# FFN gate and up in a two-layer decoder trunk: x as the stationary operand in 512-column blocks, and the results turned to channels by 32x32 transposes and copies between quadrants

## The chip, the cores and the metric

The kernel runs on one core of a Trainium2 chip. Its engines work side by side, each on its own queue of instructions: TensorE (PE; PEld is its load of the stationary operand), VectorE (DVE), ScalarE (ACT), GpSimd (POOL) and SyncE (SP, which here issues most of the transfers). The metric is the time of one execution on the device, in microseconds. A difference of about 0.2% (5.5 us) is what a measurement of this kernel can tell from no change.

## The reference, cut to what matters

The trunk has two layers with different mixers. Behind each mixer stands the same gated FFN with a causal convolution of three taps over the 256 positions of the sequence, for each of its 5120 channels:

```python
D_MODEL, SEQ, DEPTH, D_FF, FFN_CONV = 2048, 256, 2, 5120, 3

def causal_dwconv(x, w):
    K = w.shape[0]
    L = x.shape[1]
    xp = jnp.pad(x, ((0, 0), (K - 1, 0), (0, 0)))
    return sum(xp[:, j:j + L] * w[j] for j in range(K))

def conv_glu(x, w_gate, w_up, conv_w, w_down):
    gate = causal_dwconv(x @ w_gate, conv_w)
    return (jax.nn.silu(gate) * (x @ w_up)) @ w_down

for i in range(DEPTH):
    h = gdn_mixer(...) if i == 0 else dsa_mixer(...)
    x = layer_norm(DN_ALPHA * x + h, ln1_g[i], ln1_b[i])
    f = conv_glu(x, ffn_w_gate[i], ffn_w_up[i], ffn_conv_w[i], ffn_w_down[i])
    x = layer_norm(DN_ALPHA * x + f, ln2_g[i], ln2_b[i])
    x = x + jax.nn.sigmoid(x @ ple_w_gate[i]) * (p[i] @ ple_w_proj[i])
```

## The kernel before

All inputs are float32. Each product is made of three products of rounded parts: a number is split into hi (rounded to the format that PE multiplies) and lo (what is left), and hi x hi, hi x lo and lo x hi are added up in PSUM.

Weights come as blocks of 512 KB, 128 partitions by 1024 numbers. For each block, `weigh` plans four steps: SP issues the load into `raw` (L418), ACT rounds it to `hi` (L424; the planner may give this to DVE as a cast, L428), DVE subtracts to `lo` (L432), and PE multiplies. There are three buffers each of raw, hi and lo; hi and lo of a block come free when PE has finished it. x, normed and transposed, stays in `xT`: for each of the 16 k (128 rows of the model dimension) hi and lo side by side, 2 x 256 positions.

`column` makes the blocks of some columns of a weight. It has two forms. In the wide form (`wide=True`, L347 to L357, 256 columns, blocks of 4 k) the weights are stationary: for each k and each 128 columns, one matmul of hi against the 512 numbers of x's hi and lo (L357), one of lo against the 256 of x's hi (L354). The result has channels on partitions; its two halves must be added. In the other form (512 columns, blocks of 2 k) x is stationary: for each k and each 128 positions, L367 and L368 multiply x's hi and x's lo with 512 columns of hi, and L370 x's hi with 512 columns of lo. The result has positions on partitions. The down product, the output products and some others have this form already. Gate and up are wide, since the convolution runs over positions, which must then lie in a row.

`ffn` plans what follows a column of gate and of up. For each 128 channels of gate: ACT copies one half of the result (`fold`, L1540), DVE adds the other and writes `fpd` (the join, L1542; two zeros stand in front), ACT multiplies by the last tap into `fac` (L1564), DVE adds the other two taps (L1567), ACT takes silu (L1570). For up: fold and join into `fh`, DVE multiplies with `fac` (L1583), ACT rounds the product into `hTA` or `hTB` (L1585), DVE subtracts for its lo (L1587). hTA and hTB are the stationary operand of down.

The order on each engine is set when the program is built. Every step is added to `Plan` with an engine, an assumed cost, its predecessors, the buffers that it takes and gives back, and a rank; `Plan.run` goes through an assumed time and takes for each engine the step that can start, by rank. Some steps name a second engine (`other`) that may take them. On the chip each engine keeps to that order. `rest` plans both layers from the output product of the mixer on: the norm (its pairs of k are turned by PE, L1473, and written to xT), gate and up in turn, the affine part of the norm on x (L1518), down, the norm behind it and the last product.

In the opening, x and the first four blocks come in pieces. Of x's first four k, one k, one k and two k; of the first block too, which ACT's queue loads while SP loads x. Four warm-up matmuls on zeros (`spin`, L270) go ahead on PE.

## Time and profile before

| | us |
|---|---|
| median of three runs | 2734.23 (2733.2 to 2734.66) |
| the profiled execution: its time | 2730.83 |
| its span in the profile | 2729.0 |
| PE busy in the span | 2718.1 |
| DVE busy | 1903.1 |
| ACT busy | 1464.6 |
| POOL busy | 236.2 |

The span is what the profile shows from the first to the last instruction; the execution's own time has 1.8 us around it. An engine's busy time is the union of its instructions. PE's instructions overlap (a matmul starts before the one in front has ended), so a matmul's rate is read from the starts of many in a row and not from the duration of one. The mean granted clock of TensorE was 0.999 of full speed.

### The profile page before, as it was taken

How to read it: one execution, taken by the hardware profiler on the slowest of the kernel's cores; microseconds unless marked ns; L12 is line 12 of the kernel's file. 1: busy time of each engine (PE TensorE's matmuls, PEld its weight loads, DVE VectorE, ACT ScalarE, POOL GpSimd, SP SyncE). 2: the span in 40 equal slices, each digit the busy share in tenths (PEclk: the TensorE clock that was granted, in tenths of full speed). 3: DMA queues.
4: the chain of work that ended last, by engine and by line, in shares of the span. 5: the costliest groups of instructions: out<-in, count | busy, mean ns of one | idle time of the engine just before them, and what ended most of it. 6: DMA issues, size and time to landing. Idle time of an engine off the chain costs nothing.

```text
span 2729.0 us, 39745 instructions
## 1 busy us (share of the span) xinstructions
PE 2718.1 (100%) x14686; PEld 2353.3 (86%) x14686; DVE 1903.1 (70%) x3077; ACT 1464.6 (54%) x2393; POOL 236.2 (9%) x415
## 2 busy tenths in 40 slices
...
DVE  7988789777787766666446866787766666655575
...
GB/s 245 230 253 174 183 185 187 196 177 165 171 184 177 212 199 201 205 199 191 194 194 240 149 195 208 182 151 193 167 189 197 193 198 193 196 193 190 213 173 189
DMA packets 415378, 527.56 MB, mean 193 GB/s; under 512 B 24848, under 2 KB 305280, under 8 KB 414928
## 3 DMA queue, kind: packets, MB, share of 16 engines
...
q10 hardware_dynamic: 560, 0.52, 0.1%
...
## 4 chain that ended last, share of the span: by engine, by line
PE 97%; DMA 1%; DVE 1%; POOL 1%; issue 0%; ACT 0%; ACTq 0%; SPq 0%; DVEq 0%
PE mm_ps L357 34%; PE mm_ps L354 18%; PE b_ps L367 13%; PE b_ps L370 13%; PE b_ps L368 13%; PE mm_ps L351 1%; PE o_ps L1266 1%; PE s_ps L1226 0%; PE n_ps L1473 0%; PE s_ps L1141 0%; PE o_ps L1265 0%; PE l_ps L919 0%; PE ot_ps L1305 0%; DMA raw<-in_gdn_w_in 0%; PE g_ps L1119 0%; PE s_ps L1242 0%
## 5 line engine op out<-in xcount | busy, mean ns | idle before, releaser
L432 DVE TENSOR_TENSOR lo<-raw,hi 128x1024 fp32r<-128x1024 f32 (+1 forms) x903 | 1099.8, 1219 | 664.1 <-ACT hi L424 653.2
L424 ACT ACTIVATE hi<-raw 128x1024 fp32r<-128x1024 f32 (+1 forms) x877 | 923.8, 1054 | 1069.1 <-PE mm_ps L357 454.6
L357 PE MATMUL mm_ps<-xT,hi 128*128 128x512 f32 x4056 | 991.6, 393 | 3.0 <-ACT hi L462 2.7
L357 PEld LDWEIGHTS mm_ps<-xT,hi 128*128 128x128 f32 x4056 | 741.7, 189 | 146.2 <-ACT hi L462 3.2
L354 PEld LDWEIGHTS mm_ps<-xT,lo 128*128 128x128 f32 x4056 | 522.2, 191 | 20.3 <-DVE lo L432 0.4
L354 PE MATMUL mm_ps<-xT,lo 128*128 128x256 f32 x4056 | 533.3, 283 | 0.2 <-DVE lo L432 0.2
L367 PE MATMUL b_ps<-hi,xT 128*128 128x512 f32 (+2 forms) x678 | 259.8, 384 | 0.0
L368 PE MATMUL b_ps<-hi,xT 128*128 128x512 f32 (+2 forms) x678 | 257.4, 380 | 0.0
L367 PE MATMUL b_ps<-hi,hTA 128*128 128x512 f32 x512 | 199.2, 389 | 0.0
L368 PE MATMUL b_ps<-hi,hTA 128*128 128x512 f32 x512 | 199.2, 389 | 0.0
L370 PE MATMUL b_ps<-lo,xT 128*128 128x512 f32 (+2 forms) x678 | 180.4, 382 | 0.0
L368 PEld LDWEIGHTS b_ps<-hi,xT 128*128 128x128 f32 x678 | 127.4, 188 | 22.8
L367 PEld LDWEIGHTS b_ps<-hi,xT 128*128 128x128 f32 x678 | 127.4, 188 | 22.8
L370 PEld LDWEIGHTS b_ps<-lo,xT 128*128 128x128 f32 x678 | 124.4, 188 | 22.6
L370 PE MATMUL b_ps<-lo,hTA 128*128 128x512 f32 x512 | 136.8, 389 | 0.0
L1512 POOL DMA_DIRECT2D lng<-in_ln_g x16 | 8.7, 543 | 1351.0 <-DVE x L1518 1267.1
L368 PEld LDWEIGHTS b_ps<-hi,hTA 128*128 128x128 f32 x512 | 96.1, 188 | 20.0
L367 PEld LDWEIGHTS b_ps<-hi,hTA 128*128 128x128 f32 x512 | 96.1, 188 | 20.0
L370 PEld LDWEIGHTS b_ps<-lo,hTA 128*128 128x128 f32 x512 | 96.1, 188 | 20.0
L367 PE MATMUL b_ps<-hi,oT 128*128 128x512 f32 (+1 forms) x258 | 102.2, 396 | 0.8 <-ACT hi L424 0.8
L368 PE MATMUL b_ps<-hi,oT 128*128 128x512 f32 (+1 forms) x258 | 100.3, 389 | 0.0
L598 DVE SCALAR_TENSOR_TENSOR ac<-pd,cw,ac 128x256 f32<-128x256 f32 x192 | 90.5, 481 | 3.3
...
## 6 DMA issues: line engine op xcount, KB each, us to landing
raw<-in_gdn_w_in SPq DMA_DIRECT2D x188, 512.0 KB, 4.3
raw<-in_ffn_w_down SPq DMA_DIRECT2D x160, 512.0 KB, 4.1
raw<-in_ffn_w_up SPq DMA_DIRECT2D x158, 512.0 KB, 4.1
raw<-in_ffn_w_gate SPq DMA_DIRECT2D x157, 512.0 KB, 4.2
raw<-in_dsa_w_in SPq DMA_DIRECT2D x72, 512.0 KB, 3.6
raw<-in_gdn_w_o SPq DMA_DIRECT2D x64, 512.0 KB, 4.0
raw<-in_ple_w_gate SPq DMA_DIRECT2D x56, 512.0 KB, 4.2
raw<-in_dsa_w_o SPq DMA_DIRECT2D x32, 512.0 KB, 4.4
```

The costliest lines, as they stand in the source:

```text
L351: nc.tensor.matmul(ps[o][:m, :S], (hi if kind == "hi" else lo)[:, k, o * P:o * P + m], xk[:, j], start=s and not j and kind == "hi", stop= ...
L354: nc.tensor.matmul(ps[o][:m, S:], lo[:, k, o * P:o * P + m], xk[:, 0], start=False, stop=e)
L357: nc.tensor.matmul(ps[o][:m], hi[:, k, o * P:o * P + m], xk.rearrange("p a b -> p (a b)"), start=s, stop=e)
L367: nc.tensor.matmul(ps[o][:, c], xh, hi[:, k, c], start=s, stop=False)
L368: nc.tensor.matmul(ps[o][:, c], xl, hi[:, k, c], start=False, stop=False)
L370: nc.tensor.matmul(ps[o][:, c], xh, lo[:, k, c], start=False, stop=e and c.stop == n)
L424: nc.scalar.activation(hi, box["raw"], AF.Copy)
L432: nc.vector.tensor_tensor(lo, box["raw"], box["hi"].bitcast(F32), op=ALU.subtract)
L598: nc.vector.scalar_tensor_tensor(box["ac"], box["pd"][:, k:k + S], wt[:, k:k + 1], box["ac"], op0=ALU.mult, op1=ALU.add)
L1266: nc.tensor.matmul(ps[:, h], qd()[:, h, a], u()[:, a, h], start=not a, stop=True)
L1512: d = add(G, 0.55, lambda r=r, src=src: nc.gpsimd.dma_start(out=r(), in_=bass.AP(tensor=src.tensor, offset=src.offset + nb * 512, ap=[[0, ...
```

## The change

Gate and up take the form with x stationary, in columns of 512: gate(n0) and up(n0) now make four times 128 channels each, from blocks of 2 k by 512 columns. The result has positions on partitions, 2 x 128 of them by 512 channels, in two PSUM banks. `turned` brings it to channels on partitions: DVE transposes each bank in blocks of 32x32 into `xb` (`flip`), and 16 copies of 32 partitions by 256 numbers move the blocks from quadrant b of the partitions to quadrant q of `fpd`, which holds four times 2 + 256 numbers a partition. The copies are planned half for DVE and half for ACT, each with the other engine as second choice. Behind them the taps stay at 256 numbers each; silu, the product with gate, the rounding and the subtraction take 1024 numbers at once. fpd exists once and serves gate and up in turn, fac once. fold and join go.

xb becomes one tile whose halves the norm and the last product use in turn (`half_`). The first gate and up columns of a layer run block by block in turn. The blocks that are made ahead of the first norm in layer 0 are planned at other places.

In the opening the pieces of x and of the first block are 2 k each (256 KB), and six warm-up matmuls run instead of four.

```diff
-                                fac=3, fh=2, xb=2, lng=1, lnb=1, qi=2, rl=2, qq=2, pr=2, prT=2, qs=1, ks=2)
+                                fac=1, fp=1, xb=2, lng=1, lnb=1, qi=2, rl=2, qq=2, pr=2, prT=2, qs=1, ks=2)
...
-        add(E, 3.6, lambda: spin(4, True), take=["bk"], give=["bk"], rank=-9)
+        add(E, 4.9, lambda: spin(6, True), take=["bk"], give=["bk"], rank=-9)
...
-            k1 = 4 * nb
-            for n in (2, 2) if nb else (1, 1, 2):
-                k0, k1 = k1, k1 + n
-                ks = slice(k0, k1)
+            n = 2
+            for k0 in range(4 * nb, 4 * nb + 4, n):
+                ks = slice(k0, k0 + n)
...
-                xs.extend([[f]] * n)
+                xs.extend([[f]] * (n // 2))
...
-                parts = ((0, 1), (1, 2), (2, 4)) if not i else ((0, 2), (2, 4))
-                for j, (j0, j1) in enumerate(parts):
...
-                        (nc.sync if i else nc.scalar).dma_start(out=box["raw"][:, j0:j1],
-                                          in_=b["src"][b["rows"] + j0 * P:b["rows"] + j1 * P, c0:c0 + n]
+                        (nc.sync if i else nc.scalar).dma_start(out=box["raw"][:, 2 * j:2 * j + 2],
+                                          in_=b["src"][b["rows"] + 2 * j * P:b["rows"] + (2 * j + 2) * P, c0:c0 + n]
...
-                    if i or j > 1:
-                        h.append(add(A, 0.13 + 0.25 * w, high, [d], take=["hi"] * (not j), rank=0, behind=h[:j] + xs[3] * (i == 1),
-                                     other=(V, 0.11 + 0.14 * w, cast, lambda: R["cast0"])))
+                    if i or j:
+                        h.append(add(A, 0.63, high, [d], take=["hi"] * (not j), rank=0, behind=h[:j] + xs[1] * (i == 1),
+                                     other=(V, 0.39, cast, lambda: R["cast0"])))
                     else:
...
-                if kind == "hi" and b is order[0]:
-                    r += [(kind, ks[:1]), (kind, ks[1:2]), (kind, ks[2:])]
-                    continue
...
+        xb = {}
+
+        def halves():
+            if id(self.area) not in xb:
+                xb[id(self.area)] = self.area, new("xb", [2, 512])
+            return xb[id(self.area)][1]
+
+        def half_():
+            xb["n"] = xb.get("n", 1) + 1
+            return halves()[:, xb["n"] % 2]
...
-            fp = [lazy(lambda n=n: new(f"fpd{n}", [2 + S])) for n in range(2)]
-
...
-            hT = lambda k: (w["hA"](k, 1) if k < 32 else w["hB"](k - 32, 1))[:, 0]
+            fp = lazy(lambda: new("fpd", [4, 2 + S]))
+            clear = add(G, 0.3, lambda: nc.gpsimd.memset(fp()[:, :, 0:2], 0.0), [opened])
+            hT = lambda k, n=1: w["hA"](k, n) if k < 32 else w["hB"](k - 32, n)
             G_, hd = {}, {}
+
+            def turned(state, task):
+                box, d, r = {}, [], []
+
+                def flip(a):
+                    if not a:
+                        box["t"] = halves()
+                    nc.vector.transpose(box["t"][:, a], state["ps"][a])
+                for a in range(2):
+                    d.append(add(V, 0.72, lambda a=a: flip(a), [task], take=["xb"] * 2 * (not a), give=["mm"], rank=1,
+                                 behind=d[:1]))
+
+                def ends(b, q):
+                    return (fp()[32 * q:32 * q + 32, :, 2:].rearrange("p t (o b i) -> p o t b i", b=4, i=32)[:, :, :, b],
+                            box["t"][32 * b:32 * b + 32].rearrange("p o (t q i) -> p o t q i", q=4, i=32)[:, :, :, q])
+
+                def move_v(b, q):
+                    nc.vector.tensor_copy(*ends(b, q))
+
+                def move_a(b, q):
+                    nc.scalar.activation(*ends(b, q), AF.Copy)
+                for b in range(4):
+                    for q in range(4):
+                        v, c = ((lambda f=f, b=b, q=q: f(b, q)) for f in (move_v, move_a))
+                        how = (V, 0.25, v), (A, 0.4, c)
+                        one, two_ = how if (b + q) % 2 else how[::-1]
+                        r.append(add(*one, [*d, clear], take=["fp"] * (not r), rank=1.5, behind=r[:1],
+                                     other=(*two_, lambda: R["move"])))
+                return r
 
             def gate(n0):
                 def done(state, task):
                     soon = marked()
-                    for n in range(2):
-                        pd, m = fp[n], n0 + n
-                        ac = lazy(lambda: new("fac", [S], 3))
-                        x = folded(state, n, task, lambda pd=pd: pd()[:, 2:], take=["pd"], more=[clear])
-                        x = add(A, 0.5, lambda pd=pd, ac=ac, m=m: nc.scalar.activation(
-                            ac(), pd()[:, 2:], AF.Identity, scale=w["taps"](2, m)), [x, w["cw"]], take=["fac"], rank=2)
+                    ac = lazy(lambda: new("fac", [4, S]))
+                    moved, x = turned(state, task), []
+                    for n in range(4):
+                        m = n0 + n
+                        y = add(A, 0.5, lambda ac=ac, n=n, m=m: nc.scalar.activation(
+                            ac()[:, n], fp()[:, n, 2:], AF.Identity, scale=w["taps"](2, m)), [*moved, w["cw"]],
+                            take=["fac"] * (not n), give=["xb"] * 2 * (not n), rank=2)
                         for k in (1, 0):
-                            x = add(V, 0.48, lambda k=k, pd=pd, ac=ac, m=m: nc.vector.scalar_tensor_tensor(
-                                ac(), pd()[:, k:k + S], w["taps"](k, m), ac(), op0=ALU.mult, op1=ALU.add), [x],
-                                give=["pd"] * (not k), rank=soon)
-                        G_[m] = add(A, 0.41, lambda ac=ac: nc.scalar.activation(ac(), ac(), AF.Silu), [x], rank=2,
-                                    table="silu"), ac
-                return column(t["ffn_w_gate"][i], 0, n0 * P, 256, KT, lambda k: self.xT[:, k], True,
+                            y = add(V, 0.48, lambda k=k, ac=ac, n=n, m=m: nc.vector.scalar_tensor_tensor(
+                                ac()[:, n], fp()[:, n, k:k + S], w["taps"](k, m), ac()[:, n], op0=ALU.mult, op1=ALU.add), [y],
+                                rank=soon)
+                        x.append(y)
+                    G_[n0] = add(A, 1.07, lambda ac=ac: nc.scalar.activation(ac(), ac(), AF.Silu), x, give=["fp"], rank=2,
+                                 table="silu"), ac
+                return column(t["ffn_w_gate"][i], 0, n0 * P, 512, KT, lambda k: self.xT[:, k], False,
             def up(n0):
                 def done(state, task):
                     soon = marked()
-                    for n in range(2):
-                        m = n0 + n
-                        fh = lazy(lambda: new("fh", [S], 2))
-                        x = folded(state, n, task, fh, take=["fh"])
-                        d, ac = G_[m]
-                        x = add(V, 0.42, lambda fh=fh, ac=ac: nc.vector.tensor_tensor(fh(), fh(), ac(), op=ALU.mult), [x, d],
-                                give=["fac"], rank=soon)
-                        x = add(A, 0.41, lambda fh=fh, m=m: nc.scalar.activation(hT(m)[:, 0], fh(), AF.Copy), [x, w["big"]],
-                                rank=2.5)
-                        hd[m] = add(V, 0.42, lambda fh=fh, m=m: nc.vector.tensor_tensor(
-                            hT(m)[:, 1], fh(), hT(m)[:, 0].bitcast(F32), op=ALU.subtract), [x], give=["fh"], rank=soon)
-                return column(t["ffn_w_up"][i], 0, n0 * P, 256, KT, lambda k: self.xT[:, k], True,
+                    fh = lambda: fp()[:, :, 2:]
+                    d, ac = G_[n0]
+                    x = add(V, 1.25, lambda ac=ac: nc.vector.tensor_tensor(fh(), fh(), ac(), op=ALU.mult),
+                            [*turned(state, task), d], give=["fac", "xb", "xb"], rank=soon)
+                    x = add(A, 1.07, lambda: nc.scalar.activation(hT(n0, 4)[:, :, 0], fh(), AF.Copy), [x, w["big"]], rank=2.5)
+                    x = add(V, 1.25, lambda: nc.vector.tensor_tensor(
+                        hT(n0, 4)[:, :, 1], fh(), hT(n0, 4)[:, :, 0].bitcast(F32), op=ALU.subtract), [x], give=["fp"], rank=soon)
+                    hd.update((n0 + n, x) for n in range(4))
+                return column(t["ffn_w_up"][i], 0, n0 * P, 512, KT, lambda k: self.xT[:, k], False,
...
-                    blocks += [first[0][0], first[1][0], first[0][1], first[1][1]][:1]
+                    blocks += first[0][:1]
...
-                run(c, ahead_(range(16, 28, 2) if i else (9, 10, 11, 12), blocks, homes, lambda n, deps=deps: deps))
+                run(c, ahead_(range(16, 28, 2) if i else (10, 12, 14), blocks, homes, lambda n, deps=deps: deps))
...
-                for j, (a, b) in enumerate(zip(*first)):
-                    if j < R["weave"]:
-                        weave(a, b)
-                    else:
-                        run((a, b))
-                for n in range(2, D_FF // P, 2):
+                run(two(*first))
+                for n in range(4, D_FF // P, 4):
                     run(gate(n))
                     run(up(n))
```

The next rows are DVE's order in layer 0, early in gate and up, from the join of one gate column to the subtraction for the up column that follows. Rows show the line, the operation, the tiles and the size, and the count of equal neighbours; lo is the weights' split, L1518 the affine of x. First before:

```order
L1542 TENSOR_TENSOR fpd_8395<-mm_ps,fold 128x256
L1542 TENSOR_TENSOR fpd_8397<-mm_ps,fold 128x256
L432 TENSOR_TENSOR lo<-raw,hi 128x1024
L1567 SCALAR_TENSOR_TENSOR fac<-fpd_8395,fcw,fac 128x256 x2
L1567 SCALAR_TENSOR_TENSOR fac<-fpd_8397,fcw,fac 128x256 x2
L432 TENSOR_TENSOR lo<-raw,hi 128x1024 x3
L1542 TENSOR_TENSOR fh<-mm_ps,fold 128x256 x2
L1583 TENSOR_TENSOR fh<-fh,fac 128x256 x2
L432 TENSOR_TENSOR lo<-raw,hi 128x1024
L1587 TENSOR_TENSOR hTA<-fh,hTA 128x256 x2
```

And a gate column in the changed kernel, from its transposes to the last subtraction ahead of those of the up column, where b_ps is the product in PSUM and L428 a weight block's rounding on DVE:

```order
L1562 STREAM_TRANSPOSE xb<-b_ps 128x512 x2
L432 TENSOR_TENSOR lo<-raw,hi 128x1024
L1572 COPY fpd<-xb 32x2x4x32 x8
L428 CAST hi<-raw 128x1024
L432 TENSOR_TENSOR lo<-raw,hi 128x1024
L1596 SCALAR_TENSOR_TENSOR fac<-fpd,fcw,fac 128x256 x4
L432 TENSOR_TENSOR lo<-raw,hi 128x1024 x2
L1596 SCALAR_TENSOR_TENSOR fac<-fpd,fcw,fac 128x256 x3
L432 TENSOR_TENSOR lo<-raw,hi 128x1024
L1596 SCALAR_TENSOR_TENSOR fac<-fpd,fcw,fac 128x256
L432 TENSOR_TENSOR lo<-raw,hi 128x1024 x3
```

Two joins have become two transposes and eight copies, and a rounding of weights that was ACT's stands behind the copies.

On ACT, the same place (hi is the rounding of weights). Before:

```order
L1540 ACTIVATE fold<-mm_ps 128x256 x2
L424 ACTIVATE hi<-raw 128x1024
L1564 ACTIVATE fac<-fpd_8395,fcw 128x256
L1564 ACTIVATE fac<-fpd_8397,fcw 128x256
L424 ACTIVATE hi<-raw 128x1024
L1570 ACTIVATE fac<-fac 128x256 x2
L424 ACTIVATE hi<-raw 128x1024 x2
```

In the changed kernel, for a gate column and the up column behind it:

```order
L1575 ACTIVATE fpd<-xb 32x2x4x32 x8
L1592 ACTIVATE fac<-fpd,fcw 128x256 x4
L424 ACTIVATE hi<-raw 128x1024 x4
L1600 ACTIVATE fac<-fac 128x1024
L424 ACTIVATE hi<-raw 128x1024 x3
L1575 ACTIVATE fpd<-xb 32x2x4x32 x8
L424 ACTIVATE hi<-raw 128x1024 x2
L1612 ACTIVATE hTA<-fpd 128x4x256
```

Eight copies and four first taps now stand in a row on ACT, where one or two instructions stood between two roundings of weights.

## Rows read from the trace of the kernel before

**Rows 1.** The page: busy time of each engine with its share of the span and its instructions, and DVE's busy tenths in 40 equal slices of the span.

```profile
PE 2718.1 (100%) x14686; PEld 2353.3 (86%) x14686; DVE 1903.1 (70%) x3077; ACT 1464.6 (54%) x2393; POOL 236.2 (9%) x415
...
DVE  7988789777787766666446866787766666655575
```

**Rows 2.** The waits of PE over the whole span, longest in total first: who waited for whom, us in total, times, the longest.

```profile
PE mm_ps L357 <- ACT hi L462: 2.7, 1, 2.7
PE w_ps L270 <- DVE pd L257: 1.2, 1, 1.2
PE b_ps L367 <- ACT hi L424: 0.8, 1, 0.8
```

**Rows 3.** PE's timeline at the ends of the stages: start, us until the end of the group, line, result and operands, size, count. The first matmuls of gate and up in layer 0, of down in layer 0, of the product behind down, of gate and up in layer 1, of down in layer 1.

```profile
835.65 1.20 PE L357 MATMUL mm_ps<-xT,hTA 128*128 128x512 f32 x4
...
1284.24 0.39 PE L367 MATMUL b_ps<-hi,hTA 128*128 128x512 f32 x1
...
1501.91 0.40 PE L367 MATMUL b_ps<-hTA,pT 128*128 128x512 f32 x1
...
1960.26 1.20 PE L357 MATMUL mm_ps<-xT,xT 128*128 128x512 f32 x4
...
2407.89 0.39 PE L367 MATMUL b_ps<-hi,hTA 128*128 128x512 f32 x1
```

**Rows 4.** Busy time in the stretch of gate and up in layer 0: its length, then PE, PEld, DVE, ACT, POOL busy us with their instructions, granted clock, DMA share, GB/s.

```profile
835.65:1284.24 448.59, 448.59 (x2579) 395.48 (x2579) 297.64 (x428) 239.02 (x368) 10.20 (x19) 1.00 0.64 200
```

**Rows 5.** Who waited for the matmuls of L357 between 780 and 1320 us: us in total, times.

```profile
  ACT hi L424: 152.8, 112
```

**Rows 6.** PE's timeline in the middle of gate and up in layer 0 (columns as in rows 3).

```profile
892.73 3.82 PE L357 MATMUL mm_ps<-xT,hi 128*128 128x512 f32 x16
896.38 2.08 PE L354 MATMUL mm_ps<-xT,lo 128*128 128x256 f32 x16
898.30 3.82 PE L357 MATMUL mm_ps<-xT,hi 128*128 128x512 f32 x16
...
920.56 3.82 PE L357 MATMUL mm_ps<-xT,hi 128*128 128x512 f32 x16
```

**Rows 7.** PE's timeline in the first stage (columns as in rows 3): the starts of two blocks with x stationary and of the wide block behind them.

```profile
66.47 0.39 PE L367 MATMUL b_ps<-hi,xT 128*128 128x512 f32 x1
...
69.19 0.39 PE L367 MATMUL b_ps<-hi,xT 128*128 128x512 f32 x1
...
71.91 1.98 PE L357 MATMUL mm_ps<-xT,hi 128*128 128x512 f32 x8
```

**Rows 8.** Groups by line and shape over the whole span, DVE's and then ACT's: line, engine, operation, result and operands, sizes, count, busy us, mean ns of one, idle us of the engine before them and what ended it.

```profile
L1567 DVE SCALAR_TENSOR_TENSOR fac<-fpd,fcw,fac 128x256 f32<-128x256 f32 x160 | 74.1, 482 | 2.6
L1583 DVE TENSOR_TENSOR fh<-fh,fac 128x256 f32<-128x256 f32 x80 | 30.2, 417 | 0.1
L1542 DVE TENSOR_TENSOR fpd<-mm_ps,fold 128x256 f32<-128x256 f32 x80 | 30.0, 418 | 11.6 <-ACT fold L1540 11.6
...
L1540 ACT ACTIVATE fold<-mm_ps 128x256 f32<-128x256 f32 x196 | 63.1, 373 | 2.2 <-PE mm_ps L354 1.0 <-PE mm_ps L357 1.0 <-issue 0.2
L1564 ACT ACTIVATE fac<-fpd,fcw 128x256 f32<-128x256 f32 x80 | 35.9, 496 | 2.9 <-DVE fpd L1542 2.9
L1570 ACT ACTIVATE fac<-fac 128x256 f32<-128x256 f32 x80 | 29.7, 404 | 4.3 <-DVE fac L1567 4.1
L1585 ACT ACTIVATE hTA<-fh 128x256 fp32r<-128x256 f32 x64 | 24.3, 418 | 15.9 <-DVE fh L1583 15.7
```

**Rows 9.** The same view: the rows nearest to the new operations, and the rounding on ACT and on DVE and the subtraction of a weight block.

```profile
L432 DVE TENSOR_TENSOR lo<-raw,hi 128x1024 fp32r<-128x1024 f32 x887 | 1085.5, 1225 | 659.3 <-ACT hi L424 649.6 <-PE s_ps L1226 2.1 <-PE b_ps L368 1.9
L428 DVE CAST hi<-raw 128x1024 fp32r<-128x1024 f32 x27 | 18.8, 697 | 13.8 <-PE b_ps L368 6.4 <-PE mm_ps L357 4.8 <-DMA raw<-in_gdn_w_in 2.5
L855 DVE STREAM_TRANSPOSE xt<-sq 128x256 f32<-128x256 f32 x16 | 7.1, 442 | 0.3
L1052 DVE STREAM_TRANSPOSE LT<-L 64x512 f32<-64x512 f32 x8 | 5.7, 709 | 0.3
L466 DVE CAST hi<-raw 128x256 fp32r<-128x256 f32 x2 | 0.6, 290 | 3.0 <-DMA raw<-in_gdn_w_in 3.0
...
L424 ACT ACTIVATE hi<-raw 128x1024 fp32r<-128x1024 f32 x860 | 911.1, 1060 | 1048.6 <-PE mm_ps L357 450.6 <-PE b_ps L368 361.2 <-issue 61.2
```

**Rows 10.** ACT's timeline in gate and up, two instructions of 128x256 in a row.

```profile
909.30 0.75 ACT L1585 ACTIVATE hTA<-fh 128x256 fp32r<-128x256 f32 x2 [0.52 <-DVE fh L1583]
```

**Rows 11.** The page: issues of transfers, KB each, median us from issue to landing.

```profile
raw<-in_ffn_w_gate SPq DMA_DIRECT2D x157, 512.0 KB, 4.2
```

**Rows 12.** The opening on all engines (columns as in rows 3; in brackets the engine's idle time before and what ended it).

```profile
1.19 3.78 PE L270 MATMUL w_ps<-pd 128*128 128x256 f32 x8 [1.19 <-DVE pd L257]
...
4.86 1.82 PE L357 MATMUL mm_ps<-xT,hi 128*128 128x512 f32 x4
...
8.73 1.67 ACT L462 ACTIVATE hi<-raw 128x512 fp32r<-128x512 f32 x3 [0.49 <-DMA raw<-in_gdn_w_in]
...
9.41 1.87 PE L357 MATMUL mm_ps<-xT,hi 128*128 128x512 f32 x4 [2.73 <-ACT hi L462]
```

**Rows 13.** Stretches of the opening (columns as in rows 4: the granted clock and the DMA share are the second and third from the end).

```profile
9.41:11.09 1.68, 1.68 (x5) 1.29 (x5) 1.68 (x4) 1.64 (x4) 0.00 (x0) 0.58 1.04 356
11.09:12.79 1.70, 1.70 (x9) 1.70 (x8) 1.70 (x4) 1.52 (x3) 0.00 (x0) 0.50 0.98 330
```

45 lines of the change are left out of this document (20 added, 25 removed).

## Prediction

> **What bounds the kernel now.** I read the page's busy times first: PE is busy 2718.1 us of a span of 2729.0 us, DVE 70%, ACT 54% [rows 1]. Next the waits of PE, the longest first: one of 2.7 us and one of 1.2 us, both in the opening, and none of 1 us behind them [rows 2]. So no engine and no transfer holds TensorE up, and the time is the length of its stream of matmuls. A change to it is worth what it takes out of that stream, minus any wait that it puts in.
>
> The stage that is changed lies, in layer 0, between its first matmul at 835.65 and the first of the down product at 1284.24, and in layer 1 between 1960.26 and 2407.89 [rows 3]: 448.6 and 447.6 us. In layer 0's, DVE is busy 297.64 us (66%), ACT 239.02 us (53%) [rows 4]. In the stretch around layer 0's stage, ACT's rounding of a weight block (hi) waited 112 times, 152.8 us in all, for these matmuls to free a buffer [rows 5]: the weights are ahead of PE, not behind.
>
> **The rate, and what the change takes out of it.** A block is 512 KB of weights. Gate and up are 2 x 2 x 2048 x 5120 x 4 bytes, 320 blocks. Before, a block is 8 matmuls over 512 columns (hi against x's two parts) and 8 over 256 (lo). In the middle of the stage two blocks take 892.73 to 898.30, and ten take 27.83 us, up to 920.56: 2.783 us a block. In it, 16 hi take 3.65 us (228 ns each) and 16 lo 1.92 us (120 ns) [rows 6].
>
> After, a block is 12 matmuls over 512 columns, the form that down already has: 80 blocks between 1284.24 and 1501.91 make 2.721 us a block [rows 3]. x itself as the stationary operand, between wide blocks of the first stage, shows the same: two blocks start at 66.47 and 69.19, and the next wide one at 71.91 [rows 7].
>
> Both forms stream 6144 columns. The difference is per matmul: 256 columns more cost 228 - 120 = 108 ns, so each matmul costs some 12 ns beyond its columns, and four fewer save 0.048 us; the rest of the 0.062 is the switch between hi and lo. I take the measured difference: 0.062 x 320 = **19.8 us**. That is nearly all the stage has to give: 160 blocks at 2.783 are 445.3 of 448.6 us, and the rest holds turns of the norm on PE.
>
> Against this speaks the Trainium skill, "TensorE: Matmul & The Clock Gate", section "Back-to-back issue gap": a warm matmul takes N/2.4 + 2.5 ns. By it, an estimate, a block is 2.600 us before and 2.590 after, and the gain 3.3 us. The rows at 228 and 120 ns do not agree with it.
>
> **What the change adds on DVE and ACT.** For 512 columns of gate and the same of up, before [rows 8]: on DVE 8 joins (0.417), 8 taps (0.482), 4 products and 4 subtractions (0.418), 10.5 us; on ACT 8 folds (0.373), 4 first taps (0.496), 4 silu (0.404), 4 roundings (0.419), 8.3 us. After: 4 transposes of 128x512, 32 copies of 32x256, the same taps, and products, subtractions, silu and rounding as one 128x1024 instruction each.
>
> No row shows a 128x512 transpose out of PSUM. From SBUF, 64x512 took 0.709 and 128x256 0.442 [rows 9]. The lower end is the 64x512, the upper one twice that. I take 0.71: between 256 elements on 128 partitions and 512 on 64 it rises by 1.04 ns an element, so the elements in a partition seem to set it and not the number of partitions; and the join out of PSUM cost no more (0.418) than the product from SBUF (0.417). No row shows a strided 32x256 copy either. On DVE it lies between the 128x256 cast (0.29) [rows 9] and a two-operand 128x256 (0.42); it has one operand, so I take 0.29. On ACT it lies between the 0.375 that each of two in a row took (0.75) [rows 10] and the single 0.42 [rows 8]; I take the first, since eight stand in a row.
>
> Half of the copies on each engine: DVE 2.84 + 4.64 + 3.86 + 2.45 = 13.8 us a pair of columns, ACT 6.0 + 2.0 + 2.1 = 10.1. Over 10 pairs a layer DVE gains 33 us, and 14 more as it takes over one rounding (0.70) a column, as the order shows: some 345 of 438 us, 79%. ACT loses what DVE takes over. Both still have room on average, so the sum charges nothing for the work itself. What counts is the burst.
>
> **The burst at a column's end.** Call T the end of a column. PE goes on with block 1 of the next; the buffers of the block just ended come free for block 3, which PE wants 2 x 2.72 = 5.44 us later. Behind T stand on DVE, in the order, two transposes (1.42, perhaps behind a running lo), 8 copies (2.32), then the cast for block 3 (0.70): done at T + 4.5, 0.9 us early. On ACT: 8 copies behind the transposes (T + 4.5), four first taps (2.0), then hi for block 4 (1.06): T + 7.6, wanted at 8.16. So both chains just fit, the cover is 0.6 to 0.9 us, and I charge 1.0 us in all for columns where a lo or the affine of x stands in front. If the copies cost 0.42 the cast ends at T + 5.6: 0.15 late, 6 us over 40 columns.
>
> What else is late when: PSUM. The column's two banks are free after the transposes and wanted again a column later, 21.8 us. The single buffer fpd must be free of gate when up's copies come, 21.8 us later; copies, taps and silu need 3.8 + 3.9 + 1.1 us of DVE and ACT plus the lo's between, about half of that. hT: the last up column's chain (1.4 + 2.3 + 1.2 + 1.1 + 1.2 us) is wanted by down's k = 36, 18 blocks or 49 us on. These cost nothing; without the cover, a few us once a layer. Loads keep their size (512 KB, 4.2 us to landing for gate [rows 11]); SP issues as many as before. POOL's two memsets become one.
>
> **The opening.** Now 4 products start at 4.86, then PE stands until 9.41 for the second half of the first block (256 KB, landed at 8.73) [rows 12]. Afterwards that half is loaded by the same instruction, one issue earlier. The first half comes as one piece, and six warm-up matmuls instead of four (8 records in 3.78 us [rows 12], so 12 in 5.67) hold PE to 6.86; the 4 products (1.82) then end at 8.7, still before 9.41. So the later start costs nothing, with the 2.7 us wait as its cover. A gain can come from the clock: from 9.41 to 12.79 the granted clock was 0.58 and 0.50 [rows 13], and with a shorter gap before it the fast level may come earlier: at most half of 3.4 us, 1.7, and less where the transfers still set the pace, which filled the DMA engines then (1.04 and 0.98) [rows 13]. I take 0.4 of the 0 to 1.7.
>
> **Sum.** -19.8 (rate) + 1.0 (bursts) - 0.4 (opening) = -19.2 us. The profiled execution took 2730.83 us, 1.8 more than its span; it becomes 2711.6. It lay 3.4 under the median of the three runs, 2734.23; the change applies to that as well: **2715.0 us**.
>
> **Rivals.**
> (a) *Bursts starve PE: slower.* Mechanism: the cast and hi behind the transposes and copies come after PE wants them, each column. For it: the chains leave less than 1 us, and two of their prices are not in the trace. Against: hi waits for PE's buffers now, and where DVE was fullest (9 tenths of a slice [rows 1]) PE shows no wait of a us. It eats the gain from 19.8 / 40 = 0.5 us late per column, a burst 1.4 us longer than worked out. At the upper prices (transposes 1.42, copies 0.42) it is 6.2 instead of 3.74 us: 1.55 late, 62 us over 40 columns, 2776 us.
> (b) *Bursts take part of the gain.* Copies at 0.42, or lo and affine in front at most columns: 6 to 14 us lost, 2721 to 2728.
> (c) *The saving does not follow the matmul count: no change.* If the 12 ns were not a cost per matmul but of this stage, and stayed in it, only the switches would go: 0.062 - 4 x 0.012 = 0.014 us a block, 4.5 us at most, 2730 to 2734. Against it stand the x-stationary groups in the first stage, under a fuller DVE, at 2.72. The Trainium skill's rule above is this rival.
>
> **How the numbers follow.** The forecast, 2709 to 2720, gets 0.82, (b) 0.07, (c) 0.05, (a) 0.06. The lower end is the full rate gain with no burst, the whole 1.7 of the opening, and 3 us by which runs already differ from the profiled one; the upper end of the range reaches into (b), 2727. Within 0.2% (5.5 us, about what a measurement here can tell from no change) is (c) with a little of (a) and (b): 0.06; slower 0.05; faster 0.89.
>
> **What would show it.** Right: groups of 12 matmuls 2.72 us apart in gate and up; each stage about 438.5 us; DVE near 79% there; PE's waits on hi and lo still a few us in all. The transposes at 0.7, DVE's copies at 0.2 to 0.3, ACT's below 0.42. Wrong if PE waits for hi or lo shortly after each column's end, by 0.5 us or more, which is (a); or if the groups stand 2.78 apart with no wait, which is (c). The opening is judged by when the second block's products start, 12.79 now.

## The result and the profile after

The changed kernel took 2718.85 us (median of four runs, 2712.76 to 2720.04) against 2733.72 us for the kernel before beside it: ratio 0.9942, 95% interval 0.9924 to 0.9959. The forecast was 2715.0 us, 0.9930 of the 2734.23 us measured before the change. The profiled execution is the fastest of the four: 2712.76 us, its span 2711.0 us.

The page of the changed kernel, busy time as in [rows 1]. Its lines are numbered differently: L366, L367, L369 are the products with x stationary, L1562 the transposes, L1572 and L1575 the copies on DVE and ACT.

```profile
PE 2698.3 (100%) x13410; PEld 2286.1 (84%) x13410; DVE 2002.3 (74%) x3228; ACT 1498.4 (55%) x2398; POOL 237.1 (9%) x413
```

PE lost 1276 instructions (4 of a block's 16, 320 times; the two more warm-up products add four records) and 19.8 us, DVE gained 99 us. The waits of PE, as in [rows 2]:

```profile
PE b_ps L366 <- ACT hi L424: 2.9, 2, 1.6
PE s_ps L979 <- DMA Tb<-tu: 1.5, 1, 1.5
PE w_ps L271 <- DVE pd L258: 1.2, 1, 1.2
PE mm_ps L356 <- DVE xT L311: 0.8, 1, 0.8
```

The first lies in layer 0's gate and up and is new there. The second is there before too, with 0.2 us. The kernel before had one wait of the first kind as well, of 0.8 us [rows 2], in the output product of layer 0's mixer, which runs up to the first norm:

```profile
813.77 0.50 PE L367 MATMUL b_ps<-hi,oT 128*128 128x512 f32 x1 [0.83 <-ACT hi L424]
```

It is gone after the change. From the last product o_ps of the mixer to the first of gate and up, the three traces with the old gate and up take 58.56 to 58.66 us, the eleven with the new one 56.9: 1.7 us gained outside the stage. In the traces with the wait, ACT rounds a block made ahead from gate's weights (hTA<-pw) just before this hi, and the change plans these blocks at other places; no run moves them alone, so that this is the reason is not shown.

The stage edges, as in [rows 3] (gate and up, down and the product behind it in layer 0, gate and up and down in layer 1):

```profile
833.25 0.48 PE L366 MATMUL b_ps<-hTA,xT 128*128 128x512 f32 x1
...
1275.31 0.39 PE L366 MATMUL b_ps<-hi,hTA 128*128 128x512 f32 x1
...
1494.24 0.39 PE L366 MATMUL b_ps<-hTA,pT 128*128 128x512 f32 x1
...
1952.27 0.48 PE L366 MATMUL b_ps<-xT,xT 128*128 128x512 f32 x1
...
2389.70 0.39 PE L366 MATMUL b_ps<-hi,hTA 128*128 128x512 f32 x1
```

From these edges, and the same ones of the experiments below, the lengths in us:

| stretch | before | after | e9 | e12 |
|---|---|---|---|---|
| start to gate, layer 0 | 835.65 | 833.25 | 835.73 | 833.82 |
| gate and up, layer 0 | 448.59 | 442.06 | 438.33 | 438.24 |
| down, layer 0 | 217.67 | 218.93 | 217.67 | 217.67 |
| from there to gate, layer 1 | 458.35 | 458.03 | 458.05 | 458.04 |
| gate and up, layer 1 | 447.63 | 437.43 | 437.35 | 437.27 |
| down, layer 1 | 218.98 | 219.07 | 218.98 | 217.67 |

Three things are to be explained: 10.2 us gained in layer 1's gate and up but 6.5 in layer 0's; 1.26 us lost in layer 0's down; and the start, which varies most from run to run. Apart from the start a stretch that an experiment leaves alone repeats within 0.4 us from trace to trace (once within 0.7, between the layers of e1), so one trace decides about a difference of 1 us or more.

The rate itself, in layer 1 of the changed kernel (columns as in [rows 6]): one block's lo starts at 2100.48, the next one's at 2103.20, 2.72 us apart, as predicted.

```profile
2100.48 1.07 PE L369 MATMUL b_ps<-lo,xT 128*128 128x512 f32 x4
2101.39 0.39 PE L366 MATMUL b_ps<-hi,xT 128*128 128x512 f32 x1
...
2103.20 1.07 PE L369 MATMUL b_ps<-lo,xT 128*128 128x512 f32 x4
```

Busy time in gate and up of both layers of the changed kernel (columns as in [rows 4]): DVE 77% and 78%; PE lacks 2.95 us in layer 0 and nothing in layer 1.

```profile
833.25:1275.31 442.06, 439.11 (x1941) 361.99 (x1940) 341.56 (x498) 256.07 (x371) 10.21 (x19) 1.00 0.65 203
1952.27:2389.70 437.43, 437.43 (x1939) 362.10 (x1938) 341.10 (x499) 251.18 (x364) 4.29 (x8) 1.00 0.62 193
```

The new operations in its groups (columns as in [rows 8]):

```profile
L1572 DVE COPY fpd<-xb 32x256 f32<-32x256 f32 x321 | 91.4, 285 | 5.2
L1562 DVE STREAM_TRANSPOSE xb<-b_ps 128x512 f32<-128x512 f32 x80 | 52.9, 696 | 38.4 <-PE b_ps L369 38.4
L1575 ACT ACTIVATE fpd<-xb 32x256 f32<-32x256 f32 x319 | 132.7, 416 | 29.2 <-DVE xb L1562 24.0 <-DVE hTA L1613 1.9
```

### The profile page after: what moved, and what is told of

Same layout as the page of the kernel before. It is cut to its first block, busy times and chain, and to the rows that moved or that the text cites. A ratio compares the mean times of both kernels' runs of the same rounds, so it can differ in the third digit from the quotient of the medians.

```text
span 2711.0 us, 37233 instructions
## 1 busy us (share of the span) xinstructions
PE 2698.3 (100%) x13410; PEld 2286.1 (84%) x13410; DVE 2002.3 (74%) x3228; ACT 1498.4 (55%) x2398; POOL 237.1 (9%) x413
## 4 chain that ended last, share of the span: by engine, by line
PE 95%; DMA 2%; DVE 1%; issue 0%; ACT 0%; POOL 0%; SPq 0%; DVEq 0%; ACTq 0%
PE b_ps L366 24%; PE b_ps L369 24%; PE b_ps L367 24%; PE mm_ps L356 12%; PE mm_ps L353 6%; DMA raw<-in_gdn_w_in 1%; DMA raw<-in_ffn_w_gate 1%; DVE lo L432 1%; PE n_ps L1476 1%; PE o_ps L1258 1%; PE s_ps L1218 0%; PE s_ps L1133 0%; PE o_ps L1257 0%; PE l_ps L911 0%; PE ot_ps L1297 0%
## 5 line engine op out<-in xcount | busy, mean ns | idle before, releaser
L424 ACT ACTIVATE hi<-raw 128x1024 fp32r<-128x1024 f32 (+1 forms) x843 | 885.4, 1053 | 984.2 <-PE b_ps L367 499.3
L366 PE MATMUL b_ps<-hi,xT 128*128 128x512 f32 (+1 forms) x1938 | 750.8, 388 | 3.1 <-ACT hi L424 2.9
L367 PE MATMUL b_ps<-hi,xT 128*128 128x512 f32 (+1 forms) x1938 | 747.6, 386 | 0.0
L369 PE MATMUL b_ps<-lo,xT 128*128 128x512 f32 (+1 forms) x1938 | 517.2, 387 | 0.0
L366 PEld LDWEIGHTS b_ps<-hi,xT 128*128 128x128 f32 x1938 | 364.0, 188 | 77.2 <-ACT hi L424 4.9
L367 PEld LDWEIGHTS b_ps<-hi,xT 128*128 128x128 f32 x1938 | 363.9, 188 | 71.7
L369 PEld LDWEIGHTS b_ps<-lo,xT 128*128 128x128 f32 x1938 | 361.0, 188 | 71.8
L356 PE MATMUL mm_ps<-xT,hi 128*128 128x512 f32 x1536 | 387.5, 394 | 1.0 <-DVE xT L311 0.8
L356 PEld LDWEIGHTS mm_ps<-xT,hi 128*128 128x128 f32 x1536 | 278.0, 188 | 52.7 <-ACT hi L459 1.2
L353 PE MATMUL mm_ps<-xT,lo 128*128 128x256 f32 x1536 | 205.2, 284 | 0.2 <-DVE lo L432 0.2
L353 PEld LDWEIGHTS mm_ps<-xT,lo 128*128 128x128 f32 x1536 | 198.1, 191 | 7.9 <-DVE lo L432 0.4
L366 PE MATMUL b_ps<-hi,hTA 128*128 128x512 f32 x512 | 199.2, 389 | 0.0
L367 PE MATMUL b_ps<-hi,hTA 128*128 128x512 f32 x512 | 199.2, 389 | 0.0
L1575 ACT ACTIVATE fpd<-xb 32x256 f32<-32x256 f32 x319 | 132.7, 416 | 29.2 <-DVE xb L1562 24.0
L369 PE MATMUL b_ps<-lo,hTA 128*128 128x512 f32 x512 | 136.9, 389 | 0.0
L367 PEld LDWEIGHTS b_ps<-hi,hTA 128*128 128x128 f32 x512 | 96.1, 188 | 20.0
L366 PEld LDWEIGHTS b_ps<-hi,hTA 128*128 128x128 f32 x512 | 96.1, 188 | 20.0
L369 PEld LDWEIGHTS b_ps<-lo,hTA 128*128 128x128 f32 x512 | 96.1, 188 | 19.9
L366 PE MATMUL b_ps<-hi,oT 128*128 128x512 f32 (+1 forms) x258 | 102.1, 396 | 0.0
L367 PE MATMUL b_ps<-hi,oT 128*128 128x512 f32 (+1 forms) x258 | 100.3, 389 | 0.0
```

The lines of the kernel that those rows point to most:

```text
L353: nc.tensor.matmul(ps[o][:m, S:], lo[:, k, o * P:o * P + m], xk[:, 0], start=False, stop=e)
L356: nc.tensor.matmul(ps[o][:m], hi[:, k, o * P:o * P + m], xk.rearrange("p a b -> p (a b)"), start=s, stop=e)
L366: nc.tensor.matmul(ps[o][:, c], xh, hi[:, k, c], start=s, stop=False)
L367: nc.tensor.matmul(ps[o][:, c], xl, hi[:, k, c], start=False, stop=False)
L369: nc.tensor.matmul(ps[o][:, c], xh, lo[:, k, c], start=False, stop=e and c.stop == n)
L424: nc.scalar.activation(hi, box["raw"], AF.Copy)
```

## Experiments: the two parts, and the copies

**e1, the changed kernel again; e2, gate and up alone; e3, the opening alone.** e2 takes back the opening's pieces and its two additional warm-up products, e3 everything else. The line of each that says most:

```diff
 e2, against the changed kernel
-        add(E, 4.9, lambda: spin(6, True), take=["bk"], give=["bk"], rank=-9)
+        add(E, 3.6, lambda: spin(4, True), take=["bk"], give=["bk"], rank=-9)
 e3, against the kernel before
-            for n in (2, 2) if nb else (1, 1, 2):
+            n = 2
```

> The changed kernel once more, for its spread and a second trace. The four executions lay at 2712.8, 2717.7, 2720.0 and 2720.0 us with a mean granted clock of 1.000, 0.999, 0.998 and 0.997. Theory A (two places in layer 0's gate and up, behind the stores of fx, where PE waits for a weight block that landed late; 2.9 us in the trace at hand): this second trace shows waits of PE there again, of 3 to 8 us, and the time follows them. Theory B (the clock of the opening): the waits there stay near 3 us, and the slower executions have the lower clock in the first 20 us. Median expected 2716 to 2720 us by either.

> The kernel before with the FFN part of the change alone; the opening stays in pieces of one, one and two k with four warm-up matmuls. Theory B: without the new opening the executions lie close together, as those of before did (2732.4 to 2734.7), at 2733.7 - 16.7 = 2717 us. Theory A: they spread as those of the changed kernel do, and the median is 2718 to 2723 us, 2 to 3 us above the changed kernel's, which is what the opening gave in the trace (835.65 against 833.25 us at the start of gate and up).

> The kernel before with the new opening alone (pieces of two k, six warm-up matmuls). The trace of the changed kernel stood 2.4 us ahead at the start of gate and up, so 2.4 us are expected here, 2731.3 us. Theory B: executions spread by several us, as those of the changed kernel. Theory A: they lie as close together as those of before.

e1: 2716.91 us, ratio 0.9938 (0.9925 to 0.9950). e2: 2716.34, 0.9938 (0.9924 to 0.9951). e3: 2731.85, 0.9991 (0.9982 to 1.0000). The gain is that of gate and up: both layers of e2 are as long as after (442.34, 437.44). The times do not settle the opening's part: e3's interval reaches 1.0000, and e2 without the new opening is as fast as e1 with it; it is taken up below. In e1 layer 0's gate and up take 442.21 us and PE waits 3.1 us there (2.9 after), so e1's long execution (2720.1 us) does not come from this stage; its low clock is not in the first 20 us either, but at 192.8 us (below).

**e4, no turn.** The transposes and the 16 copies are left out; two DVE copies a column bring the product as it stands into fpd, with positions still on partitions.

```diff
-                    nc.vector.transpose(box["t"][:, a], state["ps"][a])
+                    nc.vector.tensor_copy(fp()[:, 2 * a:2 * a + 2, 2:], state["ps"][a].rearrange("p (t s) -> p t s", t=2))
```

> The changed kernel without the turn to channels: DVE copies each PSUM bank straight to fpd (two copies of 128x512, 0.69 us each) and transposes, xb and the 16 copies are left out, so the FFN gets its channels in a wrong arrangement. PE's stream is the same. If the burst behind each column is what delays weights (theory A in the form: lo comes late, so raw comes free late, so the load starts late), PE's waits for hi in layer 0 vanish, its stage falls from 442.1 to about 438.5 us, and the kernel gains about 3.5 us on the changed one. If the stores of fx alone do it, whatever stands on DVE, the waits stay at 3 us and the time is the changed kernel's within 1 us.

e4: 2711.96 us, ratio 0.9919 (0.9905 to 0.9932). Layer 0's gate and up fall to 438.25, layer 1's stay at 437.43. So the turning costs 3.8 us in one layer and nothing in the other, though both turn the same 20 columns. Down stays at 218.93: its 1.26 us have another cause.

**Where the 3.8 us are.** In layer 0 of the changed kernel the distance from one block's lo to the next is 2.72 us almost throughout. Behind the norm it is longer at four places: 3.69 at 867.01, 3.11 at 938.70, 4.31 at 1012.53, 4.59 at 1101.17. The first is the product f_ps among the blocks (the same in e4, and the 0.96 us by which layer 0 was longer than layer 1 before); it spreads the relative distances that layer 1's bias needs, and its result goes out by the eight stores fx. The other three are 0.39 + 1.59 + 1.87 = 3.85 us too long. The stretch before the last, on DVE, ACT, POOL and PE of the changed kernel (columns as in [rows 12]):

```profile
1080.02 2.37 DVE L1572 COPY fpd<-xb 32x256 f32<-32x256 f32 x8
...
1088.47 1.92 DVE L1596 SCALAR_TENSOR_TENSOR fac<-fpd,fcw,fac 128x256 f32<-128x256 f32 x4
1090.30 1.29 DVE L1521 TENSOR_TENSOR x<-x,lng 128x512 f32<-128x512 f32 x2
1090.42 1.06 ACT L1600 ACTIVATE fac<-fac 128x1024 f32<-128x1024 f32 x1 [4.31 <-DVE fac L1596]
1091.39 3.08 ACT L424 ACTIVATE hi<-raw 128x1024 fp32r<-128x1024 f32 x3
1091.51 1.29 DVE L1521 TENSOR_TENSOR x<-x,lnb 128x512 f32<-128x512 f32 x2
1092.71 3.49 DVE L432 TENSOR_TENSOR lo<-raw,hi 128x1024 fp32r<-128x1024 f32 x3
1093.09 0.54 POOL L1515 DMA_DIRECT2D lnb<-in_ln_b  x1 [0.65 <-DVE x L1521]
1093.63 1.06 POOL L1642 DMA_DIRECT2D fx<-fd  x2
...
1101.17 1.07 PE L369 MATMUL b_ps<-lo,xT 128*128 128x512 f32 x4
1102.69 1.06 ACT L424 ACTIVATE hi<-raw 128x1024 fp32r<-128x1024 f32 x1 [8.22 <-DMA raw<-in_ffn_w_gate]
...
1103.80 0.50 PE L366 MATMUL b_ps<-hi,xT 128*128 128x512 f32 x1 [1.57 <-ACT hi L424]
```

Read downwards. Behind the copies and the lo's between, DVE ends the taps only at 1090.39; ACT's silu waits 4.31 us for them, and hi for three blocks stands behind it. So three hi and then three lo run in a row, and the three raw buffers come free late and close together. SP, whose next load needs one of them, waits up to 4.9 us for a lo there (3.1 us in e4). Just then POOL, which the affine rows' buffers had held, issues its rows and two stores fx (256 KB and 383 KB each). The next weights land with ACT idle for 8.22 us, and PE waits. None of it is the predicted chain (cast and hi for blocks 3 and 4 behind the copies). The loads of weights issued from 1088 to 1106 us, in the changed kernel and in e9 below, which has no store there (KB each, median us from issue to landing):

```profile
raw<-in_ffn_w_gate SPq DMA_DIRECT2D x5, 512.0 KB, 8.6
```

```profile
raw<-in_ffn_w_gate SPq DMA_DIRECT2D x6, 512.0 KB, 5.6
```

In e4, with the same two stores but no turning, they take 5.7.

## Experiments: the stores

**e6, the stores in down.** rel_bias, f_ps and the eight stores are moved behind down's columns.

```diff
-                    stored = distances(opened, at)
+                    stored = distances(opened, lambda j: seq[n0 + 162 + 8 * j]["task"])
```

> The changed kernel with the spreading of the relative distances (their three small loads, one product, one copy and the eight stores fx) moved from the first layer's gate and up into its down projection. Theory: gate and up of the first layer are 4 to 5 us longer than those of the second because a group of copies delays the low parts, these give the raw weights back late, and the load of the next piece then goes beside a store fx and lands late; the second layer has no such stores: expected 437.5 to 438.5 in the first layer instead of 442.1, and the waits of ACT for the raw weights there under 40 us instead of 90. Rival: the copies or the loads of the affine rows alone do it, and the first layer stays at 442. The down stage may take some of it over, up to the 4 us.

Gate and up of layer 0, then its down (columns as in [rows 4]):

```profile
834.64:1271.89 437.25, 437.25 (x1939) 362.11 (x1938) 344.23 (x501) 253.91 (x367) 4.23 (x8) 1.00 0.64 195
1271.89:1496.14 224.25, 220.88 (x969) 180.29 (x968) 121.93 (x121) 89.60 (x90) 5.75 (x11) 1.00 0.69 218
```

437.25: with the turning and without the stores nothing is lost, as in layer 1. (ACT still waits 67 us for raw there, 87 in the changed kernel; under 40 was expected.) But down grew from 218.93 to 224.25, more than the 4 us allowed for. POOL, held by nothing there, issued all eight at once:

```profile
1290.13 4.16 POOL L1642 DMA_DIRECT2D fx<-fd  x8 [2.37 <-DMA fd<-oh]
```

In the trace four blocks between 1284.59 and 1314.37 take 3.68 to 4.51 us. The first, 0.96 us long of it, is f_ps, which moved too; the other three, behind the stores, lose 4.3 us. There ACT waits for the weights:

```profile
1302.75 1.06 ACT L424 ACTIVATE hi<-raw 128x1024 fp32r<-128x1024 f32 x1 [7.78 <-DMA raw<-in_ffn_w_down]
```

So in gate and up, with two stores at a time, it needs both the late lo's and the stores (e4 has the stores alone, e6 the turning alone). In down each lo before this wait follows its hi at once and none is late: eight stores at once stop PE without late lo's. That the size of the bundle makes the difference is likely; no run varies it alone.

**e9, the stores one at a time.** They go to SyncE's queue, where each stands between two loads of weights, sixteen blocks apart; hTB is aligned as in e5 below.

```diff
-                r.append(add(G, 0.54, lambda o=o: nc.gpsimd.dma_start(
+                r.append(add(Q, 0.5, lambda o=o: nc.sync.dma_start(
```

> The changed kernel with hTB at a multiple of 64 bytes again, and with the eight stores fx issued one at a time from SyncE's queue among the loads of the weights, sixteen pieces apart in the first layer's gate and up, instead of two at a time from GpSimd's queue right behind the loads of two affine rows. Theory (a copy group delays the low parts and with them the next loads; only two stores and two rows at once make such a load late enough to stop TensorE, 0.4 to 1.9 us at three places): a single store is absorbed, gate and up of the first layer take 438 to 439 us instead of 442.1 (0.95 us of the f_ps product stays), the down stages 217.7 instead of 218.9; in all some 6 us under the changed kernel, about 2710 us, ratio to the kernel before near 0.9915. Rival (any store beside a delayed load costs): eight places with 0.3 to 1 us each, the first layer stays at 441 to 444.

Gate and up of layer 0 take 438.33 us; behind the norm no block is longer than 2.77 us except at f_ps. e10 below, which has the alignment and not the new place of the stores, stays at 442.40 us, so it is the stores. At the same place as above ACT in e9 waits less, and PE not at all:

```profile
1101.16 1.06 ACT L424 ACTIVATE hi<-raw 128x1024 fp32r<-128x1024 f32 x1 [5.95 <-DMA raw<-in_ffn_w_gate]
```

The taps, the row adds, three hi and three lo before it are the same as in the changed kernel; only the two stores are gone from there. That settles that the bundle of stores stopped PE in this stage; whether it is the issue one by one or the other queue that helps was not separated. The time, 2711.8 us, ratio 0.9924 (0.9911 to 0.9938), is not distinguishable from e10's: the scatter of the start is as large as the 4 us.

## Experiments: the count of products, and the opening

**e7, the low products cut in two.** 16 products a block as before, with the new operands.

```diff
+                            if w != "hi" and src.shape[1] == D_FF:
+                                for h in range(2):
+                                    ch = slice(256 * h, 256 * h + 256)
+                                    nc.tensor.matmul(ps[o][:, ch], xh, lo[:, k, ch], start=False, stop=e and h == 1)
```

> The changed kernel with each product by the low part of gate and up cut into two of 256 columns, so that a block is again 8 products of 512 and 8 of 256 columns instead of 12 of 512: the same columns as before and after, and the number of products of the kernel before with the operands of the new one. Theory (the saving is a fixed cost of each product, some 12 to 16 ns): the second layer's gate and up go back from 437.4 to 447 to 449 us, about the 447.6 of the kernel before. Rival (the saving is not a matter of the count of products, but of which operand stands or of the loads): they stay under 440.

e7 takes 448.95 us in layer 1, 11.5 more than after and 1.3 more than before: the saving follows the count of products. (One execution, 2735.1 us in all.) PE's timeline in e7:

```profile
2101.01 1.12 PE L371 MATMUL b_ps<-lo,xT 128*128 128x256 f32 x8
2101.96 0.40 PE L366 MATMUL b_ps<-hi,xT 128*128 128x512 f32 x1
...
2103.80 1.11 PE L371 MATMUL b_ps<-lo,xT 128*128 128x256 f32 x8
```

A block takes 2.79 us instead of 2.72. Eight lo take 0.95 instead of 0.91 us for four, and the eight hi behind them 1.84 instead of 1.81, though they are the same products: with short ones among them the long ones run slower too.

**e8, four warm-up products with the 256 KB pieces.**

```diff
-        add(E, 4.9, lambda: spin(6, True), take=["bk"], give=["bk"], rank=-9)
+        add(E, 3.6, lambda: spin(4, True), take=["bk"], give=["bk"], rank=-9)
```

> The changed kernel with four warming products at the start instead of six, as in the kernel before; the 256 KB pieces stay. Theory (the opening gained 2.3 us because the second halves of the first weights and columns are there earlier, and the six products only fill what was a wait): 0 to 1 us slower than the changed kernel, the first products begin no later, at 5.7 us of the span or before. Rival (the two more products bring the clock up earlier and that is the gain): about 2 us slower, with a stretch at half clock in the opening that the changed kernel does not have. Ratio to the kernel before about 0.994 by the first, 0.9945 to 0.995 by the second.

e8: 2715.23 us, ratio 0.9944 (0.9927 to 0.9960), no different from the changed kernel. The opening of the changed kernel, as in [rows 12], and behind it e8's:

```profile
1.19 4.68 PE L271 MATMUL w_ps<-pd 128*128 128x256 f32 x12 [1.19 <-DVE pd L258]
5.66 1.19 PE L356 MATMUL mm_ps<-xT,hi 128*128 128x512 f32 x4
7.59 1.17 PE L356 MATMUL mm_ps<-xT,hi 128*128 128x512 f32 x4 [0.75 <-DVE xT L311]
8.60 1.11 PE L353 MATMUL mm_ps<-xT,lo 128*128 128x256 f32 x8
9.54 1.77 PE L356 MATMUL mm_ps<-xT,hi 128*128 128x512 f32 x7
```

```profile
5.64 3.94 PE L356 MATMUL mm_ps<-xT,hi 128*128 128x512 f32 x8 [0.67 <-DVE xT L311]
9.42 0.75 PE L353 MATMUL mm_ps<-xT,lo 128*128 128x256 f32 x5
```

With four, the first eight products still run at half pace (3.94 us); with six they do not (1.19 us for four). The profile gives a granted clock of 1.00 in both from 4 to 14 us, so these rows do not show that the pace is the clock's. Yet near 188 us both are equally far. There PE waits for a transfer into Tb, a tile of layer 0's mixer, and its place ahead of that wait is the cleanest measure of the opening: start of the row minus the wait, 187.70 in e8 and 187.75 in the changed kernel.

**e11, the kernel before once more**, for its trace.

> The kernel before once more, for its trace alone. Theory: the time of one execution depends on a wait of TensorE for the transfer that fills Tb, near 184 us of the span, in a stage that the change doesn't touch; the profiled execution of the kernel before had 0.2 us there and no fall of the clock, others have 1.5 to 3.7 us with 3.4 to 6.8 us at half clock behind it: here too some 2 us and a fall of the clock, and a first stage some 2 to 4 us longer than 835.65 us, while gate and up and down keep 448.6, 217.7 and 447.6 us.

2732.45 us; gate and up 448.74 and 447.65, down 217.67. The same row in the kernel before, in e11, after and in e1:

```profile
190.02 1.05 PE L987 MATMUL s_ps<-Gy,Tb 128*128 128x32 f32 x8 [0.18 <-DMA Tb<-tu]
```

```profile
191.33 1.05 PE L987 MATMUL s_ps<-Gy,Tb 128*128 128x32 f32 x8 [2.21 <-DMA Tb<-tu]
```

```profile
189.30 1.05 PE L979 MATMUL s_ps<-Gy,Tb 128*128 128x32 f32 x8 [1.55 <-DMA Tb<-tu]
```

```profile
192.80 1.89 PE L979 MATMUL s_ps<-Gy,Tb 128*128 128x32 f32 x8 [3.66 <-DMA Tb<-tu]
```

PE arrives at 189.84, 189.12 and (e2) 189.24 with the old pieces, mean 189.4, and at 187.5 as the mean of the eleven traces with the new ones (186.4 to 189.1): the opening gains 1.9 us. The wait then takes 0.2, 2.2 and 1.8 us with the old ones and 2.1 in the mean with the new, so 1.2 us are left behind it. Behind the wait the granted clock fell in nine of the fourteen traces: e1's stretch (columns as in [rows 13]) is at 0.52, the lower level:

```profile
192.80:199.60 6.80, 6.80 (x23) 5.88 (x24) 1.23 (x1) 3.43 (x10) 2.89 (x6) 0.52 0.53 169
```

What a fall costs is read from this row to the first product o_ps behind it: 15.5 to 15.6 us in the five traces without a fall, 17.1 to 17.2 in eight, 18.6 in e1, so 1.6 us and 3.1. The length of the wait alone does not decide: a fall followed the 1.23 us of e7, none the 2.97 of e12. With the new pieces eight of eleven traces have a fall, with the old ones one of three (e2). So how much of the opening's 1.2 us reaches the end of an execution stays open.

This place, which the change does not touch, makes up 5.2 of the 6.55 us by which the first stretch spreads between the changed kernel's trace and e1's (839.8). The two traces of the kernel before have no fall; the profiled execution, with 0.18 us of wait here, lay 3.4 us under its median. What sets the transfer's time was not tried.

## Experiments: where hTB begins

**e5 and e10, hTB aligned** (the same kernel, e10 timed). As the program is laid out, hTB begins at a multiple of 128 bytes of a partition in layer 0 of the kernel before and 32 bytes past one after the change, since other tiles beside it have other sizes now. fpd is 4128 bytes long, and where it is 32 bytes longer hTB begins 32 bytes lower.

```diff
-            fp = lazy(lambda: new("fpd", [4, 2 + S]))
+            fp = lazy(lambda: new("fpd", [4, 4 + S])[:, :, :2 + S])
```

> The changed kernel with the tile that holds the channels of gate and up two columns wider (4 x 260 instead of 4 x 258 values, 4160 bytes of a partition instead of 4128), so that the tile hTB that is allocated after it begins at an address that is a multiple of 64 bytes, as it did in the kernel before, and not 32 bytes past one; nothing else is touched. Theory: the down projection lost its 1.26 us (217.67 to 218.93) because the products that take hTB as the stationary operand then take 396 ns instead of 389 and start some 6 ns further apart: expected 217.7 in the first layer's down stage, 389 ns for these products, and some 1.3 us less in the second layer's too. Rival: the stage is longer for what the new order of the weights left behind at its start; then it stays at 218.9. Gate and up of either layer: 442.1 and 437.4 in both cases.

> The changed kernel with hTB at a multiple of 64 bytes, as e5_aligned, now timed: by its stages 1.26 us in the first down projection and the same in the second, so 2 to 3 us under the changed kernel: ratio to the kernel before 0.9925 to 0.9935.

Down in layer 0 is back at 217.67 us in both (e5 is one execution, 2711.62 us). The products with hTB stationary in that stretch, after and in e5:

```profile
L366 PE MATMUL b_ps<-hi,hTB 128*128 128x512 f32 x62 | 24.5, 396 | 0.0
```

```profile
L366 PE MATMUL b_ps<-hi,hTB 128*128 128x512 f32 x62 | 24.1, 389 | 0.0
```

e10: 2711.57 us, ratio 0.9921 (0.9909 to 0.9934). The second layer did not follow: 218.98 us, 0.09 less than after. There hTB lies 64 bytes past a multiple of 128 in e10, and so it does in the kernel before, whose second layer shows slow products too:

```profile
L367 PE MATMUL b_ps<-hi,hTB 128*128 128x512 f32 x48 | 19.1, 398 | 0.0
L368 PE MATMUL b_ps<-hi,hTB 128*128 128x512 f32 x48 | 18.9, 393 | 0.0
```

So the expectation that 64 bytes are enough fell, and 128 took its place.

**e12, aligned to 128 in both layers,** on top of e9:

```diff
-            fp = lazy(lambda: new("fpd", [4, 4 + S])[:, :, :2 + S])
+            fp = lazy(lambda: new("fpd", [4, 4 + S + 4 * i])[:, :, :2 + S])
```

> As e9_aligned_sp, with the tile of the channels wider by another 64 bytes of a partition in the second layer only, so that there too hTB begins at a multiple of 128 bytes (it lies 64 bytes past one in e9_aligned_sp and in the kernel before, and 96 past one in the changed kernel). Theory (the stationary operand must begin at a multiple of 128 bytes of a partition for 389 ns; 32, 64 and 96 past one all give 393 to 398 ns): the second layer's down projection falls from 218.98 us to 217.67, that of the first layer, and its products with hTB from 398, 393 and 395 ns to 389; the kernel about 1.3 us under e9_aligned_sp, at about 2709 us. Rival (64 bytes are enough, and the second layer's 1.31 us have another cause): it stays at 218.98.

Down in layer 1: 217.67 us, 1.31 less. Its products in e12:

```profile
L366 PE MATMUL b_ps<-hi,hTB 128*128 128x512 f32 x62 | 24.1, 389 | 0.0
L367 PE MATMUL b_ps<-hi,hTB 128*128 128x512 f32 x62 | 24.1, 389 | 0.0
```

e12: 2706.67 us, ratio 0.9902 (0.9886 to 0.9919) to the kernel before, the lowest of all. The stage shows the 1.3 us; the time lies 5.1 us under e9's, with overlapping intervals, and the rest of that is not the alignment's (its trace had no fall of the clock in the start).

## Why the prediction was right, and where it was not

The sum as it came out, from the table: rate -20.4 (10.2 a layer; layer 0's 6.5 plus the 3.85 lost there), lost blocks +3.85, down +1.35, the wait in the output product that is gone -1.7, the rest -0.3: -17.2 for gate and up. e2, which has this part alone, measured -17.8 (2716.34 against 2734.1). The opening adds -1.2 at Tb, and the falls of the clock behind it take some of that back: e1 measured -17.2, e8 -16.5, the four runs of the result -14.9; the prediction said -19.2. That 2718.85 us lies within the forecast's 2709 to 2720 (2727, which the prediction also names as an upper end, belongs to a rival) owes something to luck: 2.85 us more lost in blocks and 1.35 in down stand against 1.7 that the output product gained unforeseen and 0.6 more from the rate.

- **Bound: right.** PE stayed 100% busy, and what left its stream left the time.
- **Rate: right.** -20.4 against -19.8. The stage in layer 1 is 437.43, forecast 438.5. e7 shows the cause, the count of products; the remainder put down to the switch of hi and lo is seen in e7 as hi at 230 ns instead of 226. Rival (c) falls. By the rule of the Trainium skill, "TensorE: Matmul & The Clock Gate", section "Back-to-back issue gap" (N/2.4 + 2.5 ns, which the section gives for the gap of an isolated matmul and not for a stream of loads and matmuls), an estimate, eight lo of 256 columns would take 0.87 us and four of 512 0.86; the rows of e7 and after show 0.95 and 0.91. The gain by that rule is 3.2 us, not the 3.3 of the prediction.
- **Prices: right.** The transpose 696 ns (taken 710), the copy on DVE 285 (290); on ACT 416, not 375. The prediction put 0.15 us of lateness a column on copies at 0.42 (its own terms give 1.42 + 3.36 + 0.70 = 5.48 for the cast, 0.04 late); DVE's did not cost that, ACT's nearly did, and layer 1 loses nothing. DVE's share 77 to 78%, forecast 79.
- **Bursts: the term mis-sized and the chain wrong.** 1.0 us was charged for lo or affine standing in front; 3.85 were lost, all in layer 0. The step that failed looked at the cast and hi for the next blocks, and took the weights to be ahead of PE because hi waited for buffers [rows 5]. What it left out is that a late lo holds raw, so the load itself starts late, and that the stores POOL sends at that time make it land later (8.6 us in the median, 5.6 without them). Rival (a), lateness at every column, did not come; (b) is nearest, with another mechanism.
- **"These cost nothing": wrong for down,** by 1.26 us. The late hT was harmless, as said; the address of hTB was not looked at, though only the size of a neighbouring tile moved it.
- **The output product: not seen.** The 0.8 us wait for hi stands in [rows 2]; the prediction called no wait of 1 us a sign that nothing holds PE up, and had no term for it. 1.7 us went with it.
- **Opening: mis-sized.** 0.4 taken of 0 to 1.7; 1.9 came, of which some 1.2 outlast Tb. The second block's products start at 9.54 instead of 12.79. Six warm-up products took 4.68 us, not 5.67. The range had considered the clock alone; e8 comes as far with the eight first products at half pace, which leaves the earlier arrival of the pieces, in one trace.
- **From own time to the median: not reasoned.** The profiled execution of the kernel before was one with hardly a Tb wait and no fall of the clock; the prediction carried the 3.4 us over without naming them.
